# Turning down-projection groups and up-projection tiles of an MLP into one mixed order, with 4 of 8 pairs by seven products

## The chip, the cores and the metric

One core of a Trainium2 chip runs the whole kernel in one launch. The metric is the device time of one execution in microseconds, the median of three runs. Its five engines have queues of their own and meet at semaphores: TensorE (PE; its weight loads are a row of their own, PEld), VectorE (DVE), ScalarE (ACT), GpSimd (POOL) and SyncE (SP, which issues the loads of weights).

## The reference

Two layers over 256 tokens and 2048 features in float32. Each layer is an attention block and then an MLP with a residual:

```python
def rms_norm(x, g):
    xf = x.astype(jnp.float32)
    y = xf * lax.rsqrt(jnp.mean(xf * xf, axis=-1, keepdims=True) + EPS)
    return (y * g.astype(jnp.float32)).astype(x.dtype)

def sq_relu_mlp(h, g, w_in, w_out):
    return jnp.square(jax.nn.relu(rms_norm(h, g) @ w_in)) @ w_out

# in each layer, after attention and its output projection:
#   h = h + sq_relu_mlp(h, norm_mlp[layer], w_mlp_in[layer], w_mlp_out[layer])
# w_mlp_in: 2048 x 8192, w_mlp_out: 8192 x 2048
```

The change is in the MLP alone. The attention, the key and value projections and the output projections stay as they are.

## The kernel before

**Products.** Every matrix product is made from float32 operands split in two parts of a shorter format: `hi` is a cast (ACT), `lo` is the rest (DVE, `lo = raw - hi`). Of the four partial products three are taken, hi·hi, hi·lo and lo·hi. TensorE holds a 128x128 block still and moves up to 512 columns past it. Weights come as units of 128x1024 (512 KB): SP loads `raw`, ACT makes `hi`, DVE makes `lo`. Six `raw`, four `hi` and five `lo` buffers exist. `stream` lists all units in order, `weights()` hands out the next and keeps three more prepared.

**Up.** The MLP goes through four chunks `c` of 2048 hidden features. A chunk has 16 up tiles `f` of 128 features. An up tile takes two weight units and the normed input `xg_` (tile `mlpx`): 16 wide matmuls (`hi` weights still, 512 columns: hi and lo of the 256 tokens) and 16 narrow ones (`lo` weights, 256 columns). `two_tiles` makes two tiles together: the wide ones of both, then the narrow ones of both, or in the opposite order (`width["last"]` keeps the kind that came last, so that kinds change as seldom as possible). `features_major` makes one tile in that way. After the last matmul `low_part` copies the bank's right half (ACT, `low`, L451), `up` adds the left half (DVE, L1132) and squares the relu (DVE, L1138); `finish` multiplies by `r2`, the inverse mean square of the token (DVE, L1093), casts `hid` hi (ACT, L1094) and subtracts for `hid` lo (POOL, L1095). `r2` comes from `inverse_square`: a matmul with minus ones, a scaling and a reciprocal on DVE (L552, L553).

**Down.** When all 16 tiles of a chunk are done, `pair_group(c, n)` multiplies the chunk with the down weights, for `n` = 0 and 1, each 1024 of the 2048 outputs in two columns of 512. Here tokens stand still and weights move, 512 wide. The chunk's 16 tiles make eight pairs `j`. For each pair the block product has two token halves, two feature tiles and two columns. Directly that is 8 products (two weight units, one for each column, 12 matmuls each). By a Strassen-Winograd scheme it is 7 products in four weight steps (21 matmuls): the sums and differences of weights are made in place by DVE (`prepare_seven`, four operations on 512 columns, L222 to L226), those of the hidden values by DVE in `finish` (L1111), and both are split again. The table `SEVEN` says which pairs go by seven: 0, 2, 4 (THREE) or 0, 2, 4, 6 (FOUR), for each layer, chunk and group; `group_order` puts two or three direct units between the steps of a seven-product pair. A group's sums lie in eight PSUM banks: 11, 21, 12 and 22 in the pool `ps_mm` (which has four, shared with all up tiles and other projections), p1 and p5 in `ps_s` (two), p6 in `ps_t` and p7 in `ps_y` (one each). When a sum is complete it is copied (first chunk, mostly by ACT) or added by DVE (L1057) to `d` and `e` tiles in SBUF; in some groups ACT copies it first and DVE adds later (`staged`). `merged` combines the seven sums at the end and `turned` transposes the result on TensorE and adds it to `h` (L998).

In the last chunk only group 0 goes that way; the other two quarters of the outputs are made by `tokens_major`, and in layer 1 the last one by `features_major`.

**Order.** TensorE's instructions stay in program order (`InOrder`). On DVE, ACT and POOL the compiler's scheduler orders the instructions, by readiness and program order, once and for all; each engine then works its queue in that order and waits at the head. Side work (`later`, `start_side`) is placed by `slot()`, which is called once or twice per tile. A tile of a pool takes any free buffer of its tag, and waits if there is none.

Of the kernel before, what the change touches and what calls it, by code (L numbers as in the profile page):

```python
# [16 lines left out]
P = 128  # L17
D = 2048
T = 256
# [33 lines left out]
def group_order(sevens):  # L53


    others = [(j, col) for col in "12" for j in range(KT // 2) if j not in sevens]
    behind = (1, 2, 3) if len(sevens) == 3 else (1, 2)
    steps = []
    for j in sevens:
        for i in range(4):  # L60
            steps.append((j, i))
            if i in behind:
                steps.append(others.pop(0))
    return steps + others
# [41 lines left out]
def trunk(  # L106
# [440 lines left out]
    def inverse_square(acc, name):  # L547

        ps = ps_y.tile([P, 512], F32, name="inv", tag="y")
        mm(ps[:, :T], neg_ones[:], acc[:], True, True)  # L550
        r2 = const.tile([P, T], F32, name=f"r2_{name}", tag="r2")
        nc.vector.tensor_scalar(r2[:], ps[:, :T], -1.0 / D, EPS, op0=ALU.mult, op1=ALU.add)  # L552
        nc.vector.reciprocal(r2[:], r2[:])  # L553
        return r2
# [248 lines left out]
    def mlp_stream(l):  # L803
        for c in range(NCH):
            n = FIRST_UP if c == 0 else 0
            for h in range(2):
                for f in range(n):
                    stream.append(w_up[l, c * KT + f, h])
            for f in range(n, KT):
                for h in range(2):  # L810
                    stream.append(w_up[l, c * KT + f, h])
            def unit(g, j):
                ap = w_down[l, 4 * g : 4 * g + 4, 2 * c + j // 4]
                ap = ap[:, :, 256 * (j % 4) : 256 * (j % 4) + 256]
                return ap.rearrange("o p x -> p o x")

            for n, sevens in enumerate(SEVEN[l][c]):
                for j, step in group_order(sevens):
                    sides = [unit(2 * n + i, j) for i in range(2)]
                    if step == 0:  # L820
                        seven = Sevenfold(*sides)
                    stream.append(Gathered(sides["12".index(step)]) if step in ("1", "2") else seven)
            for g in range(2, 4) if c == NCH - 1 else ():
                if by_features(l, c, g):
                    for o in range(4 * g, 4 * g + 4):
                        for h in range(2):
                            stream.append(w_down[l, o, 2 * c + h])
                    continue
                stream.extend(Gathered(unit(g, j)) for j in range(KT // 2))
# [141 lines left out]
    def mlp(l, xg_, sq, h, done):  # L971
        inv = {}
        later(lambda: inv.update(r2=inverse_square(sq, f"mlp{l}")), 4)
# [50 lines left out]
        def pair_group(c, n, hid, factors, staged=None):  # L1024

            banks = {q: ps_mm.tile([P, 512], F32, name="acc", tag="acc") for q in ("11", "21", "12", "22")}
            banks.update((q, ps_s.tile([P, 512], F32, name="acc", tag="s")) for q in ("p1", "p5"))
            banks["p6"] = ps_t.tile([P, 512], F32, name="acc", tag="t")
            banks["p7"] = ps_y.tile([P, 512], F32, name="acc", tag="y")
            sevens = len(SEVEN[l][c][n])  # L1030
            counts = {q: [0, 3 * sevens] for q in banks}
            for q in ("11", "21", "12", "22"):
                counts[q][1] = 6 * (KT // 2 - sevens) + (3 * sevens if q != "22" else 0)

            sums_of = {
                "11": [summed(0, 2 * n)], "21": [summed(1, 2 * n)],
                "12": [summed(0, 2 * n + 1)], "22": [summed(1, 2 * n + 1)],
                "p1": [product_sum(0, n), summed(0, 2 * n)], "p6": [product_sum(0, n)],
                "p5": [product_sum(1, n)], "p7": [product_sum(2, n)],
            }  # L1040

            def add(q, a, w):
                product(banks[q], a, w, counts[q])
                if counts[q][0] < counts[q][1]:
                    return
                src = banks[q][:]
                if staged is not None and q in ("12", "22", "p1", "p5", "p6", "p7"):
# [3 lines left out]
                    staged.extend((dst, copy[:]) for dst in sums_of[q])  # L1051
                    return
                for dst in sums_of[q]:
                    if c == 0 and q not in ("11", "p6"):
# [4 lines left out]
            def tokens(kt, m):  # L1059
                return [hid[:, kt, i * T + m * P : i * T + (m + 1) * P] for i in range(2)]  # L1060

            def part(unit, k2):
                return [x[:, k2 * 512 : (k2 + 1) * 512] for x in unit]

            for j, step in group_order(SEVEN[l][c][n]):
                w = weights()
                if step in ("1", "2"):
                    for m in range(2):
                        for k2 in range(2):
                            add(f"{m + 1}{step}", tokens(2 * j + k2, m), part(w, k2))  # L1070
                    slot()
                    continue
                s = factors[j]
                pairs = [
                    (("p1", tokens(2 * j, 0)), ("11", tokens(2 * j + 1, 0))),
                    (("12", s[3]),),
                    (("p5", s[0]), ("p7", s[2])),
                    (("p6", s[1]), ("21", tokens(2 * j + 1, 1))),
                ][step]
                for k2, (q, a) in enumerate(pairs):  # L1080
                    add(q, a, part(w, k2))
                if step in (1, 3):
                    slot()

        began = clock["slot"]
        for c in range(NCH):
            hid = new_act(f"hid{l}_{c}")
            squares = {}
            factors = {}

            def finish(f, hid=hid, squares=squares, factors=factors, c=c):
                a = squares[f]
                nc.vector.tensor_tensor(a[:], a[:], inv["r2"][:], op=ALU.mult)  # L1093
                nc.scalar.copy(hid[:, f, :T], a[:])  # L1094
                nc.gpsimd.tensor_tensor(  # L1095
                    hid[:, f, T:], a[:], hid[:, f, :T].bitcast(F32), op=ALU.subtract
                )
                if f % 2 == 0 or f // 2 not in SEVEN[l][c][-1]:
                    return

                s12 = nar.tile([P, T], F32, name="s12", tag="bias", bufs=6)
                s34 = nar.tile([P, T], F32, name="s34", tag="bias", bufs=6)
                a11, a21 = squares[f - 1][:, :P], squares[f - 1][:, P:]
                a12, a22 = a[:, :P], a[:, P:]
                for out_, x0, x1, op in (
                    (s12[:, :P], a21, a22, ALU.add),
                    (s12[:, P:], s12[:, :P], a11, ALU.subtract),
                    (s34[:, :P], a11, a21, ALU.subtract),
                    (s34[:, P:], a12, s12[:, P:], ALU.subtract),
                ):  # L1110
                    nc.vector.tensor_tensor(out_, x0, x1, op=op)  # L1111
                factors[f // 2] = []
                if f // 2 < 6:
                    s_hi = wide.tile([P, 512], F32R, name="s_hi", tag="wide")
                    s_lo = wide.tile([P, 512], F32R, name="s_lo", tag="wide")
                for i, s in enumerate((s12, s34)):
                    if f // 2 < 6:
                        hi, lo = (x[:, i * T : (i + 1) * T] for x in (s_hi, s_lo))
                    else:
                        hi, lo = (  # L1120
                            nar.tile([P, T], F32R, name=name, tag="bias", bufs=6)[:]
                            for name in ("s_hi", "s_lo")
                        )
# [24 lines left out]
            for f in range(n, KT, 2):  # L1148
                two_tiles(xg_, [lambda b, i=i: up(i, b) for i in (f, f + 1)])
# [248 lines left out]
```

## Time and profile before

| | |
|---|---|
| median of 3 runs | 2166.73 us (2166.26 to 2167.32) |
| profiled execution, first to last instruction | 2165.4 us |
| TensorE busy | 2158.2 us, 11083 matmuls |
| VectorE busy | 1690.1 us |
| ScalarE busy | 1191.3 us |
| GpSimd busy | 326.7 us |
| first MLP | from 435.7 to 1126.9 us |
| second MLP | from 1470.6 us to the end |
| TensorE clock granted | 1.000 |

For the profiled execution the span from its first to its last instruction is what was kept of its own time; the timed median is 1.3 us longer. A row of the page's groups, or of the view by line, reads: line, engine, operation, output<-inputs, shapes, count | busy us, mean ns of one | idle us of the engine just before them, and what ended most of it. A row in order of time reads: start us, duration us, engine, line, operation, in brackets the idle time before it and what ended it. A row of waits reads: who <- for whom: us in total, times, longest. TensorE's matmuls are pipelined, so one takes longer than the step from start to start.

### The profile page before, as it was taken

How to read it: one execution, taken by the hardware profiler on the slowest of the kernel's cores; microseconds unless marked ns; L12 is line 12 of the kernel's file. 1: busy time of each engine (PE TensorE's matmuls, PEld its weight loads, DVE VectorE, ACT ScalarE, POOL GpSimd, SP SyncE). 2: the span in 40 equal slices, each digit the busy share in tenths (PEclk: the TensorE clock that was granted, in tenths of full speed). 3: DMA queues.
4: the chain of work that ended last, by engine and by line, in shares of the span. 5: the costliest groups of instructions: out<-in, count | busy, mean ns of one | idle time of the engine just before them, and what ended most of it. 6: DMA issues, size and time to landing. Idle time of an engine off the chain costs nothing.

```text
span 2165.4 us, 30280 instructions
## 1 busy us (share of the span) xinstructions
PE 2158.2 (100%) x11083; PEld 1852.1 (86%) x11083; DVE 1690.1 (78%) x2431; ACT 1191.3 (55%) x1668; POOL 326.7 (15%) x349
## 2 busy tenths in 40 slices
PE   9999999999999999999999999999999999999999
PEld 8888888888888888888888889888888888988887
DVE  7778885678977987997886556567797798799796
ACT  7744545555655555555555447655565556555553
POOL 0010112621001001001050112352100100100100
PEclk9999999999999999999999999999999999999999
DMA  9655556655765765666666654455676577667665
GB/s 325 197 165 185 168 179 195 198 192 166 212 205 178 208 213 178 194 219 189 202 180 191 185 190 136 131 188 183 182 201 224 164 203 223 188 180 219 190 180 156
DMA packets 213317, 414.66 MB, mean 191 GB/s; under 512 B 13232, under 2 KB 144304, under 8 KB 213168
## 3 DMA queue, kind: packets, MB, share of 16 engines
q1 hardware_dynamic: 212592, 410.63, 62.0%
q8 instruction: 87, 1.43, 0.3%
q10 hardware_dynamic: 576, 2.10, 0.3%
q14 instruction: 62, 0.51, 0.1%
HBM read 410.58 MB, written 2.10 MB: 191 GB/s over the span
## 4 chain that ended last, share of the span: by engine, by line
PE 98%; DVE 1%; DMA 0%; issue 0%; ACT 0%; SPq 0%
PE acc L77 94%; PE yp L77 1%; PE accs L77 1%; PE tp L77 1%; PE s L77 1%; PE z L77 1%; DMA raw<-in_w_mem 0%; DVE lo L176 0%; DVE pt L640 0%; DVE lo L250 0%; DVE h L998 0%; ACT hi L173 0%; DVE kvx L465 0%; ACT hi L249 0%; PE stat L77 0%
## 5 line engine op out<-in xcount | busy, mean ns | idle before, releaser
L176 DVE TENSOR_TENSOR lo<-raw,hi 128x1024 fp32r<-128x1024 f32 (+1 forms) x524 | 642.6, 1237 | 308.4 <-ACT hi L173 183.3
L173 ACT CAST hi<-raw 128x1024 fp32r<-128x1024 f32 (+1 forms) x524 | 546.4, 1045 | 375.8 <-PE acc L77 316.7
L77 PE MATMUL acc<-hi,hid 128*128 128x512 f32 x1474 | 481.4, 389 | 0.0
L77 PE MATMUL acc<-mlpx,hi 128*128 128x512 f32 x2048 | 472.6, 390 | 0.0
L77 PEld LDWEIGHTS acc<-mlpx,hi 128*128 128x128 f32 x2048 | 382.0, 188 | 77.7
L77 PEld LDWEIGHTS acc<-hi,hid 128*128 128x128 f32 x1474 | 276.7, 188 | 57.5
L77 PE MATMUL acc<-lo,hid 128*128 128x512 f32 x737 | 286.7, 389 | 0.0
L1095 POOL TENSOR_TENSOR hid<-upsq,hid 128x256 fp32r<-128x256 f32 x128 | 122.3, 964 | 1086.2 <-ACT hid L1094 1086.2
L227 ACT CAST hi<-raw 128x1024 fp32r<-128x1024 f32 x204 | 192.1, 946 | 132.8 <-PE acc L77 56.0
L77 PEld LDWEIGHTS acc<-mlpx,lo 128*128 128x128 f32 x2048 | 250.6, 192 | 2.8
L77 PE MATMUL acc<-mlpx,lo 128*128 128x256 f32 x2048 | 252.0, 283 | 0.0
L228 DVE TENSOR_TENSOR lo<-raw,hi 128x1024 fp32r<-128x1024 f32 x204 | 222.8, 1108 | 29.6 <-ACT hi L227 28.0
L249 ACT CAST hi<-raw 128x1024 fp32r<-128x1024 f32 x146 | 154.0, 1055 | 126.1 <-PE acc L77 104.5
L77 PE MATMUL acc<-hi,xg 128*128 128x512 f32 x640 | 208.4, 398 | 0.0
L250 DVE TENSOR_TENSOR lo<-raw,hi 128x1024 fp32r<-128x1024 f32 x146 | 179.2, 1228 | 14.4 <-ACT hi L249 13.7
L77 PEld LDWEIGHTS acc<-lo,hid 128*128 128x128 f32 x737 | 138.4, 188 | 28.5
L77 PEld LDWEIGHTS acc<-hi,xg 128*128 128x128 f32 x640 | 120.2, 188 | 24.6
L451 ACT COPY low<-acc 128x256 f32<-128x256 f32 x188 | 69.1, 368 | 112.2 <-PE acc L77 111.9
L77 PE MATMUL acc<-lo,xg 128*128 128x512 f32 x320 | 124.7, 390 | 0.7 <-DVE lo L176 0.7
L77 PE MATMUL acc<-y,hi 128*128 128x512 f32 x512 | 119.9, 391 | 0.0
L77 PEld LDWEIGHTS acc<-y,hi 128*128 128x128 f32 x512 | 95.0, 188 | 19.0
L1094 ACT CAST hid<-upsq 128x256 fp32r<-128x256 f32 x128 | 51.9, 407 | 75.6 <-DVE upsq L1093 75.4
(202 smaller groups left out, 2610.4 us busy)
## 6 DMA issues: line engine op xcount, KB each, us to landing
raw<-in_w_up SPq DMA_DIRECT2D x256, 512.0 KB, 4.4
raw<-in_w_down SPq DMA_DIRECT2D x256, 512.0 KB, 5.6
raw<-in_w_in SPq DMA_DIRECT2D x80, 512.0 KB, 3.7
raw<-in_w_o SPq DMA_DIRECT2D x64, 512.0 KB, 4.0
raw<-in_w_mem SPq DMA_DIRECT2D x28, 512.0 KB, 5.9
raw<-in_w_kv_v SPq DMA_DIRECT2D x24, 512.0 KB, 3.9
raw<-in_w_kv_k SPq DMA_DIRECT2D x24, 512.0 KB, 4.2
raw<-in_w_q SPq DMA_DIRECT2D x24, 512.0 KB, 4.1
```

The lines of the kernel that those rows point to most:

```text
L77: return self._tc.keep_in_program_order(fn(*args, **kwargs))
L173: nc.scalar.copy(hi[:, :n], raw[:, :n])
L176: nc.vector.tensor_tensor(lo, raw, hi.bitcast(F32), op=ALU.subtract)
L227: nc.scalar.copy(hi4, src)
L228: nc.vector.tensor_tensor(lo4, src, hi4.bitcast(F32), op=ALU.subtract)
L249: nc.scalar.copy(hi4, turned)
L250: nc.vector.tensor_tensor(lo4, turned, hi4.bitcast(F32), op=ALU.subtract)
L451: nc.scalar.copy(low[:], bank[:, T:])
L1094: nc.scalar.copy(hid[:, f, :T], a[:])
L1095: nc.gpsimd.tensor_tensor(hid[:, f, T:], a[:], hid[:, f, :T].bitcast(F32), op=ALU.subtract)
```

## The change

The MLP's steps are now written as one list, `mlp_steps`. The first two tiles of chunk 0 (H) and the next six (T, by `two_tiles`) come first. Then for each chunk and group `weave` mixes kinds of steps: `U` f is an up tile (by `features_major`), `S` j a pair by seven products, `A` j and `B` j a direct unit of the first or second column. In group 0 of a chunk (`late`) the up tiles are the chunk's own last eight; in group 1 they are the first eight of the next chunk. In every group pairs 0 to 3 go by seven and 4 to 7 directly. The orders that come out are

```
late:  U8 S0 U9 S1 U10 S2 U11 S3 U12 A4 A5 U13 U14 A6 U15 B4 B5 B6 A7 B7
other: U0 S0 A4 U1 S1 A5 U2 S2 A6 U3 S3 A7 U4 U5 B4 U6 B5 U7 B6 B7
last:  (chunk 3 has group 0 only, in the late order)
```

A bank is taken at a sum's first product, and 22 comes from `ps_s`. `hid` is one tile for all chunks of a layer. The inverse is now a root, `ri`, by a power on POOL over 128x256; relu and `ri` are applied together on DVE and ACT squares. The subtraction for `hid` lo moves from POOL to DVE. The block sums of the hidden values get new homes (some in the even tile's place in `hid`), and the even tile of a seven-product pair is no longer split by itself except in the last chunk. In layer 1, `turned(3)` moves behind the last group.

```diff
-THREE, FOUR = (0, 2, 4), (0, 2, 4, 6)
-SEVEN = [
-    [(FOUR, FOUR), (THREE, FOUR), (THREE, FOUR), (THREE,)],
-    [(FOUR, FOUR), (THREE, FOUR), (THREE, FOUR), (FOUR,)],
-]
+SEVEN = [4, 4]
+BY_TURNS = 8
+
+def weave(sevens, late):
+    first, second = [], []
+    u = BY_TURNS if late else 0
+    for j in range(sevens):
+        first += [("U", u), ("S", j)]
+        u += 1
+    direct = list(range(sevens, KT // 2))
+    last = u + BY_TURNS - sevens
+    if late:
+        a, b = list(direct), list(direct)
+        for i, f in enumerate(range(u, last)):
+            second.append(("U", f))
+            while a and 2 * a[0] + 1 < f:
+                second.append(("A", a.pop(0)))
+        second += [("B", j) for j in b[:-1]] + [("A", j) for j in a] + [("B", b[-1])]
+    else:
+        steps, first = first, []
+        a = list(direct)
+        for step in steps:
+            first.append(step)
+            if step[0] == "S" and a:
+                first.append(("A", a.pop(0)))
+        b = [("A", j) for j in a] + [("B", j) for j in direct]
+        for f in range(u, last):
+            second += [("U", f)] + ([b.pop(0)] if f > u else [])
+        second += b
+    return first + second
...
-    def inverse_square(acc, name):
+    def inverse_root(acc, name):
...
-        nc.vector.reciprocal(r2[:], r2[:])
-        return r2
+        nc.gpsimd.tensor_tensor(
+            ri[:], ri[:], neg_half[:, 0:1].to_broadcast([P, T]), op=ALU.pow
+        )
+        return ri
...
+            def bank(self, q):
+                if q not in self.banks:
+                    pool, tag = {
+                        "p1": (ps_s, "s"), "p5": (ps_s, "s"), "22": (ps_s, "s"),
+                        "p6": (ps_t, "t"), "p7": (ps_y, "y"),
+                    }.get(q, (ps_mm, "acc"))
+                    self.banks[q] = pool.tile([P, 512], F32, name="acc", tag=tag)
+                return self.banks[q]
...
-                nc.vector.tensor_tensor(a[:], a[:], inv["r2"][:], op=ALU.mult)
-                nc.scalar.copy(hid[:, f, :T], a[:])
-                nc.gpsimd.tensor_tensor(
-                    hid[:, f, T:], a[:], hid[:, f, :T].bitcast(F32), op=ALU.subtract
+        def split(hi, lo, src):
+            nc.scalar.copy(hi, src)
+            nc.vector.tensor_tensor(lo, src, hi.bitcast(F32), op=ALU.subtract)
...
+        def finish(c, f):
+            squares, factors = chunks[c]
+            a = squares[f]
+            nc.vector.scalar_tensor_tensor(
+                out=a[:], in0=a[:], scalar=0.0, in1=inv["ri"][:], op0=ALU.max, op1=ALU.mult
+            )
+            nc.scalar.activation(a[:], a[:], AF.Square)
+            if f // 2 >= sevens:
+                split(hid[:, f, :T], hid[:, f, T:], a[:])
+            elif f % 2 == 1:
+                split(hid[:, f, :T], hid[:, f, T:], a[:])
+                factors[f // 2] = block_sums(c, f // 2, squares.pop(f - 1), a)
...
+        for c, n, kind, i in mlp_steps(l):
...
+            if kind == "U":
+                features_major(xg_, lambda b, c=c, i=i: up(c, i, b))
+                continue
...
+            if kind == "S":
+                groups[c, n].seven(i)
+            else:
+                groups[c, n].direct(i, "AB".index(kind) + 1)
```

More of the change, by code (lines that the diff above doesn't have):

```diff
@@ L1022, in product @@
                 count[0] += 1
[L1024 to L1044, printed above, removed]
+        hid = new_act(f"hid{l}")
@@ new lines, in seven @@
+            def seven(self, j):
+                s = self.factors[j]
+                width["last"] = "wide"
+                for step, pairs in enumerate((
+                    (("p1", s[0]), ("11", tokens(2 * j + 1, 0))),
+                    (("12", s[4]),),
+                    (("p5", s[1]), ("p7", s[3])),
+                    (("p6", s[2]), ("21", tokens(2 * j + 1, 1))),
+                )):
+                    w = weights()
+                    for k2, (q, a) in enumerate(pairs):
+                        self.add(q, a, part(w, k2))
+                    if step in (1, 3):
+                        slot()
@@ new lines, in direct, with tokens, part @@
+            def direct(self, j, col):
+                width["last"] = "wide"
+                w = weights()
+                for m in range(2):
+                    for k2 in range(2):
+                        self.add(f"{m + 1}{col}", tokens(2 * j + k2, m), part(w, k2))
+                slot()
+        def tokens(kt, m):
+            return [hid[:, kt, i * T + m * P : i * T + (m + 1) * P] for i in range(2)]
+        def part(unit, k2):
+            return [x[:, k2 * 512 : (k2 + 1) * 512] for x in unit]
@@ new lines, in up @@
+        def up(c, f, bank):
+            early = c == 0 and f < 4
+            low = low_part(bank)
+            if early:
+                t = wide.tile([P, T], F32, name="up", tag="wide")
+            else:
+                t = nar.tile([P, T], F32, name="up", tag="nar")
+            chunks[c][0][f] = t
+            nc.vector.tensor_tensor(t[:], bank[:, :T], low[:], op=ALU.add)
+            if early:
+                later(lambda: finish(c, f), began + 11 + f - clock["slot"])
+            else:
+                finish(c, f)
@@ new lines, in down_last, with group @@
+        def down_last(o, bank):
+            nc.vector.tensor_tensor(h(o), bank[:, T:], h(o), op=ALU.add)
+            done(o)
+        def group(g, banks):
+            for m in range(2):
+                nc.vector.tensor_tensor(
+                    summed(m, g), banks[m][:], summed(m, g), op=ALU.add
+                )
+            start_side(turned(g, done))
+        for g in range(2, 4):
+            if not by_features(l, c, g):
+                tokens_major(hid, lambda b, g=g: group(g, b))
+                continue
+            for o in range(4 * g, 4 * g + 4):
+                if o == KT - 1:
+                    last_tile(
+                        hid, lambda b, o=o: down_early(o, b), lambda b, o=o: down_last(o, b)
+                    )
+                else:
+                    features_major(hid, lambda b, o=o: down(o, b))
```

304 lines of the change are left out of this document (128 added, 176 removed).

## The prediction

> **What bounds the kernel now.** I read the head of the page first, then TensorE's waits, then busy time by stage, then the order of time in two places.
>
> ```profile
> span 2165.4 us, 30280 instructions
> PE 2158.2 (100%) x11083; PEld 1852.1 (86%) x11083; DVE 1690.1 (78%) x2431; ACT 1191.3 (55%) x1668; POOL 326.7 (15%) x349
> PE 98%; DVE 1%; DMA 0%; issue 0%; ACT 0%; SPq 0%
> ...
> PE tp L77 <- DVE h L998: 1.9, 2, 1.1
> PE cold L77 <- DVE zeros L144: 1.1, 1, 1.1
> PE acc L77 <- DVE lo L176: 0.7, 1, 0.7
> PE accs L77 <- ACT hi L173: 0.4, 1, 0.4
> ```
>
> TensorE carries 98% of the chain and waits for other engines 4.1 us in all (last four rows), of which the MLPs hold the two `tp` waits. So there is next to no wait to remove: time falls only with TensorE work, and any new wait of TensorE is paid in full. Next, stages (columns: PE, PEld, DVE, ACT, POOL busy, clock, DMA share, GB/s) and TensorE at the start of the first MLP:
>
> ```profile
> 525.00:606.60 81.60, 81.60 (x361) 67.59 (x360) 76.09 (x86) 53.05 (x64) 2.95 (x2) 1.00 0.73 207
> 777.70:866.50 88.80, 88.80 (x513) 78.76 (x512) 67.75 (x108) 47.19 (x71) 12.28 (x14) 1.00 0.60 191
> 866.50:948.80 82.30, 82.30 (x364) 68.16 (x364) 77.31 (x90) 47.90 (x54) 2.81 (x2) 1.00 0.69 204
> 1037.60:1126.90 89.30, 88.18 (x401) 72.83 (x401) 77.96 (x89) 45.24 (x53) 27.17 (x25) 1.00 0.67 200
> ...
> 451.11 14.70 PE L77 MATMUL acc<-mlpx,hi 128*128 128x512 f32 x64
> 465.64 7.83 PE L77 MATMUL acc<-mlpx,lo 128*128 128x256 f32 x64
> 473.31 2.00 PE L77 MATMUL acc<-mlpx,hi 128*128 128x512 f32 x8
> ```
>
> From start to start, 64 wide products take 465.64 - 451.11 = 14.53 us, 0.227 us each, and 64 narrow ones 473.31 - 465.64 = 7.67 us, 0.120 each; the turns from wide to narrow and back lie inside and cost nothing. An up tile is 16 of each: 5.55 us (a sixteenth of the second stage's 88.80). Down groups (first and third stage) run TensorE full with DVE at 93 to 94%; up tiles (second) leave DVE at 76%.
>
> **The change part by part.**
>
> *Products.* A pair with seven products is 21 wide matmuls in place of 24. Before, 25 pairs have them in layer 0 (4+4, 3+4, 3+4, 3) and 26 in layer 1; after, 28 in each. 5 more pairs x 3 x 0.227 = 15 matmuls = -3.4 us. The clock row is 1.00 and no matmul becomes shorter, so this is all that TensorE can gain, bar the two `tp` waits (1.9 us), which I leave as they are: the transposes stand behind the same DVE adds. The Trainium skill (TensorE: Matmul & The Clock Gate, Back-to-back issue gap) gives about 131 ns per matmul at N=512 in a stream with weight loads; by it the 15 would be worth 2.0 us. This trace has 227, and the trace decides.
>
> *A wait for a PSUM bank, new.* Up tiles and the sums 11, 21 and 12 share the four banks of ps_mm. In the late order (U8 S0 U9 S1 U10 S2 U11 S3 U12 A4 A5 U13 U14 A6 U15 B4 B5 B6 A7 B7) 11 and 21 are open from S0 to A7, 12 from S0 to B7: one bank is left for up tiles. Everywhere an S or an A, 4.76 or 2.72 us of matmuls, stands between two up tiles, except U13 and U14. U14's first matmul waits until ACT has copied U13's `low` and DVE has added `up`; TensorE's order is fixed, so A6, U15 and all behind it wait too. In the other order U4 and U5 are neighbours also, but 11 and 21 closed at A7, one tile earlier. There are 4 late groups in each layer: 8 waits. The trace shows the length of that evacuation, where two free banks hide it:
>
> ```profile
> 466.85 2.36 DVE L176 TENSOR_TENSOR lo<-raw,hi 128x1024 fp32r<-128x1024 f32 x2 [3.55 <-issue]
> 467.75 0.37 ACT L451 COPY low<-acc 128x256 f32<-128x256 f32 x1 [0.82 <-PE acc L77]
> 469.13 0.42 DVE L1132 TENSOR_TENSOR up<-acc,low 128x256 f32<-128x256 f32 x1
> ...
> 455.96 0.36 ACT L451 COPY low<-acc 128x256 f32<-128x256 f32 x1
> 457.23 0.42 DVE L1132 TENSOR_TENSOR up<-acc,low 128x256 f32<-128x256 f32 x1
> ```
>
> The first tile of that narrow run issues its 16 until 465.64 + 16 x 0.120 = 467.56; `low` starts 0.19 later, DVE is held by two `lo`, `up` ends at 469.55: 2.0 us. A tile that ended wide issued until 451.11 + 16 x 0.227 = 454.74 and was out at 457.65: 2.9 us, ACT and DVE both held. With both free it is 0.19 + 0.37 + 0.42 = 1.0. Bounds 1.0 and 2.9; I take 2.0, because U13 ends narrow like the first, and A6's and U15's weights are split at just that time. 8 x 2.0 = +16.0 us (8 to 23). Between U14 and U15 A6's 2.72 us cover the 2.0.
>
> *VectorE in the mixed stretches.* Its instructions overlap a little, so I take start to start:
>
> ```profile
> 525.09 1.22 DVE L250 TENSOR_TENSOR lo<-raw,hi 128x1024 fp32r<-128x1024 f32 x1
> 526.23 0.69 DVE L225 TENSOR_TENSOR raw<-raw,raw 128x512 f32<-128x512 f32 x1
> 526.83 1.22 DVE L228 TENSOR_TENSOR lo<-raw,hi 128x1024 fp32r<-128x1024 f32 x1
> 527.97 0.42 DVE L1132 TENSOR_TENSOR up<-acc,low 128x256 f32<-128x256 f32 x1
> 528.30 0.90 DVE L226 TENSOR_TENSOR raw<-raw 128x512 f32<-128x512 f32 x1
> ...
> L1111 DVE TENSOR_TENSOR s<-upsq 128x128 f32<-128x128 f32 x30 | 20.3, 716 | 0.5
> ```
>
> A full `lo` is 1.14, a 512-wide operation 0.60, a 256-wide one 0.33. A pair of seven is 3 x 1.14 + 5 x 0.60 = 6.4 beside 4.76 of TensorE; a direct unit 1.14 beside 2.72. Before, one S goes with two A/B: 8.7 in 10.2. After, late: one S with one up tile, whose three operations stay three (the multiplication by r2 goes to ACT as a Square, the `hid` subtraction comes from POOL): 6.4 + 2 x 1.14 + 3 x 0.33 = 9.7 in 10.3, 94%, four times in a row; then up tiles with A and B at 60%. In the other order U, S and A take 6.4 + 3.4 + 0.7 = 10.5 for an even tile; an odd one has eight operations of 256 elements or fewer besides (a split, four block sums, three splits), two of them perhaps as long as the 0.72 that they took beside POOL: 2 x 0.72 + 6 x 0.33 = 3.4 more, so at most 12.2 in 13.0 on average, 94%. The first quoted stage ran at 93% with no wait, so I put it at nothing; its price without that cover is a rival. The accumulations (9 x 0.60 a group on DVE; in the first chunk ACT copies most) fall into the second halves with room.
>
> *ScalarE, POOL, DMA.* 128 Squares at 0.41 us (row L1094 below) are 52 us of ACT; it stood at 51 to 65% in the stages, so hidden, though Square now stands between two DVE operations of the same tile: the chain to `hid` is longer by about 0.8 us, and A6 first reads U13 5.5 us later. POOL loses 128 `hid` subtractions (row L1095); none of its successors waited, so no gain. Pairs read the same two raw units as their A and B: as many DMAs and bytes; SP issues them in another order, four units in 10.3 us, 203 GB/s, as in the stages above: nothing. `hid` is now one tile for all chunks; U1 writes features 0 and 1 only after S0, and each later writer follows its reader in the same way: nothing.
>
> *The inverse root.* A DVE reciprocal is replaced by a POOL power over 128x256, twice:
>
> ```profile
> 449.86 1.75 DVE L553 RECIPROCAL r_mlp<-r_mlp 128x256 f32<-128x256 f32 x1
> 451.65 0.76 DVE L1093 TENSOR_TENSOR upsq<-upsq,r_mlp 128x256 f32<-128x256 f32 x2
> 453.19 1.05 ACT L173 CAST hi<-raw 128x1024 fp32r<-128x1024 f32 x1 [0.34 <-PE acc L77]
> ...
> L571 POOL TENSOR_TENSOR sroot<-msq,neg_half x20: 1007/1012/1983, 59.5 to 1221.1; 128x4 f32<-128x4 f32 x20
> L483 POOL TENSOR_TENSOR sq<-h 128x256 f32<-128x256 f32 x45 | 48.3, 1078 | 36.0 <-DVE h L964 23.8 <-DVE h L998 12.0
> L1095 POOL TENSOR_TENSOR hid<-upsq,hid 128x256 fp32r<-128x256 f32 x64 | 61.0, 962 | 542.7 <-ACT hid L1094 542.7
> L1094 ACT CAST hid<-upsq 128x256 fp32r<-128x256 f32 x64 | 25.9, 406 | 37.3 <-DVE upsq L1093 37.2
> ```
>
> No row has this power. If its 1.0 us on 4 elements is a start-up, it costs that plus an ordinary 256-wide operation, 2 us; if it goes by element, 1.007 / 4 x 256 = 64 us. Until then DVE, and behind it ACT with its Square, stand still in their queues. TensorE has 64 wide products from 451.1; the second 32, from 458.4, need casts that began at 453.2 and took 1.05: ACT may be 4 us late. The old inverse was ready at 451.6, so a power of up to 5.8 us costs nothing, each us above it about one. I take the low end, since the row of equal shape (1.08) is the near one in size, with the other as a rival. The Trainium skill (GPSIMD Engine Reference, Performance pitfalls for Q7 kernels) says that a chain of dependent fp32 steps costs 4 cycles for each step and element unless unrolled; that speaks for the high end, and no run here shows it.
>
> **Sum.** -3.4 + 16.0 = +12.6 us on the profiled 2165.4: 2178.0. The timed median, 2166.7, lies 1.3 above the span: 2179.3.
>
> **The rivals.**
> (a) Not slower: U13's evacuation comes at once because little else is queued. At 1.0 us a wait the sum is +4.6, 2171.3; if U14 does not wait at all, 2163.3. It decides below 0.96 us a wait, where the total stays within 4.3 us (0.2%, about what a measurement of this kernel can tell from no change). For it: the second half of a late group loads DVE at 60%. Against: splits of coming weights fill any free slot, as in the quoted rows.
> (b) DVE doesn't hold 94% with up tiles between the pairs. If it gets 88% done, a late U and S take 9.7 / 0.88 = 11.0, 0.7 more, 4 x 8 times: +22, 2202. For it: subtraction, cast and `lo` of one pair alternate between DVE and ACT. Against: no wait at 93% before; three units are prepared ahead.
> (c) The power is long: at 64 us (64 - 6) x 2 = +116, 2295; at 15 us +18, 2197. For it the four-element row, against it only the shape.
>
> **How the numbers follow.** Forecast 0.45 (0.04 of it within 4.3 us), (a) 0.17, (b) 0.17, (c) 0.21, half of it above 2220. The forecast's own range is 2171 to 2187; the whole reaches from (a) to past (b) and the short powers of (c): 2163 to 2215. A gain of over 4.3 us needs more than the 3.4 of matmuls, the `tp` waits too: 0.04, out of (a). Within: the other 0.13 of (a) and 0.04 of the forecast, 0.17. Slower: 0.79.
>
> **What would show it.** 15 fewer matmuls (11068). In TensorE's waits eight of 1 to 3 us at `acc`, released by `up`, about 10 us before a late group's end. DVE 90 to 95% busy in late first halves, with no TensorE wait for `lo`. One POOL power a layer; its duration, and whether ACT or DVE stand behind it, settles (c). I am wrong if those eight waits are missing, or if waits for `lo` or `hi` exceed them.

## The result, and the profile after

The changed kernel takes 2220.18 us (2219.22 to 2223.03), the kernel before 2166.7: a ratio of 1.0249, 95% interval 1.0235 to 1.0264. That is 53.4 us slower, against 12.6 forecast, and above the range. The profiled execution spans 2221.3 us against 2165.4, 55.9 more. Lines of the changed kernel named below: `low` L475 and `up` L1186 take an up tile out of its bank; L1168 applies relu and root, L1171 squares; L1126 and L1127 are the two halves of `split`; L246 to L250 make the sums of weights and L252 their low parts; L200 is the low part of an ordinary weight unit; L1039 are the additions of `merged`.

The page: its head, its chain of waits by engine, and one of its groups:

```profile
span 2221.3 us, 30125 instructions
PE 2173.0 (98%) x11068; PEld 1854.9 (84%) x11068; DVE 1678.7 (76%) x2465; ACT 1225.1 (55%) x1784; POOL 286.2 (13%) x223
PE 91%; POOL 4%; DVE 4%; ACT 1%; issue 0%; DMA 0%; SPq 0%; ACTq 0%
...
L577 POOL TENSOR_TENSOR ri_mlp<-ri_mlp,neg_half 128x256 f32<-128x256 f32 x2 | 82.3, 41138 | 14.3 <-DVE ri_mlp L576 14.3
```

TensorE's waits:

```profile
PE acc L101 <- ACT hid L1126: 20.1, 2, 10.1
PE acc L101 <- DVE up L1186: 14.8, 10, 3.8
PE acc L101 <- DVE lo L252: 5.1, 6, 1.5
PE tp L101 <- DVE h L1023: 2.2, 2, 1.1
```

The 15 matmuls are gone. TensorE's share of the chain fell from 98 to 91%; POOL, 0% before, holds 4% by one instruction that ran twice, the power. The first three rows of waits, 40 us, are all new. The place of the largest, in order of time (selected rows):

```profile
450.28 41.14 POOL L577 TENSOR_TENSOR ri_mlp<-ri_mlp,neg_half 128x256 f32<-128x256 f32 x1 [7.14 <-DVE ri_mlp L576]
485.79 0.88 PE L101 MATMUL acc<-mlpx,lo 128*128 128x256 f32 x6
491.45 2.10 DVE L1168 SCALAR_TENSOR_TENSOR up<-up,ri_mlp 128x256 f32<-128x256 f32 x6 [3.57 <-POOL ri_mlp L577]
491.91 1.09 ACT L1171 ACTIVATE up<-up 128x256 f32<-128x256 f32 x3 [5.29 <-DVE up L1168]
496.74 0.79 PE L101 MATMUL acc<-hi,hid 128*128 128x512 f32 x1 [10.07 <-ACT hid L1126]
497.33 0.63 PE L101 MATMUL acc<-lo,hid 128*128 128x512 f32 x1
497.75 1.05 PE L101 MATMUL acc<-hi,hid 128*128 128x512 f32 x2
```

The same place by stretches (selected; columns as in the prediction):

```profile
435.70:486.60 50.90, 50.90 (x295) 45.00 (x293) 29.48 (x34) 21.49 (x27) 41.57 (x7) 1.00 0.60 176
490.00:497.00 7.00, 0.26 (x1) 0.27 (x2) 5.52 (x20) 4.13 (x13) 1.42 (x1) 0.51 0.19 71
497.00:507.00 10.00, 6.49 (x21) 4.78 (x21) 9.93 (x27) 7.82 (x18) 0.00 (x0) 0.83 0.29 70
520.00:545.00 25.00, 24.59 (x127) 20.78 (x127) 23.28 (x31) 16.93 (x25) 0.00 (x0) 1.00 0.72 202
```

Read it from the power down. It runs from 450.3 to 491.4. TensorE works on without a gap until 486.6 (first stretch: 50.90 of 50.90), through all eight first up tiles and U8; then it needs the first pair's hidden values. From the end of the power six relu-and-root operations on DVE, squares, and splits lead to `hid` at 496.74: 5.3 us. So TensorE stands still for 10.1 us. The clock follows: 0.51 in the stretch of the wait, and the next matmul is 0.42 us behind the one before it (497.33 to 497.75), where 0.227 is the full step. Then U9 waits again (3.8 us), since U8's bank is not out yet. VectorE has a backlog there: in the 40 us from 451 to 491 it was busy for 29.4 us in the kernel before and is for 20.5 now, and from 497 to 507 for 9.93 of 10.

To account for the whole I took, for every two neighbouring matmuls of the MLPs, the time from start to start less the full-clock step (0.227 wide, unrounded 0.2267, and 0.120 narrow). This excess is 2.2 us in the kernel before and 60.9 after: 58.7 more, less 3.4 for the products, is 55.3 of the 55.9. A wait counted in this way is a little longer than the idle time in the rows. Of the 60.9, 46.0 are waits, 8.5 steps at half clock and 6.4 small delays. By place: the two powers with the waits and the slow clock behind them 18.1 and 18.5; the eight waits U13 to U14 8.6; the start of chunk 3's group 3.1 of waits in the first layer, 3.5 in the second, with 2.3 of half clock there.

### The profile page after: what moved, and what is told of

Read it like the earlier page. It is cut to its first block, busy times and chain, and to the rows that moved or that the text cites. A ratio compares the mean times of both kernels' runs of the same rounds, so it can differ in the third digit from the quotient of the medians.

```text
span 2221.3 us, 30125 instructions
## 1 busy us (share of the span) xinstructions
PE 2173.0 (98%) x11068; PEld 1854.9 (84%) x11068; DVE 1678.7 (76%) x2465; ACT 1225.1 (55%) x1784; POOL 286.2 (13%) x223
## 4 chain that ended last, share of the span: by engine, by line
PE 91%; POOL 4%; DVE 4%; ACT 1%; issue 0%; DMA 0%; SPq 0%; ACTq 0%
PE acc L101 87%; POOL ri_mlp L577 4%; PE yp L101 1%; PE accs L101 1%; PE tp L101 1%; PE s L101 1%; PE z L101 1%; DVE lo L200 1%; ACT hi L197 1%; DVE lo L252 1%; DMA raw<-in_w_mem 0%; DVE up L1168 0%; ACT hi L251 0%; DVE up L1186 0%; DVE d L1039 0%
## 5 line engine op out<-in xcount | busy, mean ns | idle before, releaser
L200 DVE TENSOR_TENSOR lo<-raw,hi 128x1024 fp32r<-128x1024 f32 (+1 forms) x524 | 641.4, 1236 | 293.8 <-ACT hi L197 261.9
L101 PE MATMUL acc<-hi,hid 128*128 128x512 f32 x1520 | 506.8, 392 | 20.1 <-ACT hid L1126 20.1
L101 PE MATMUL acc<-mlpx,hi 128*128 128x512 f32 x2048 | 489.0, 392 | 7.4 <-DVE up L1186 7.4
L101 PEld LDWEIGHTS acc<-hi,hid 128*128 128x128 f32 x1520 | 287.2, 189 | 78.7 <-ACT hid L1126 20.5
L251 ACT CAST hi<-raw 128x1024 fp32r<-128x1024 f32 x224 | 211.4, 945 | 198.0 <-DVE raw L247 132.6
L101 PE MATMUL acc<-lo,hid 128*128 128x512 f32 x760 | 298.0, 392 | 0.0
L101 PEld LDWEIGHTS acc<-mlpx,lo 128*128 128x128 f32 x2048 | 260.2, 191 | 17.2 <-DVE up L1186 9.0
L101 PE MATMUL acc<-mlpx,lo 128*128 128x256 f32 x2048 | 264.9, 283 | 7.4 <-DVE up L1186 7.4
L252 DVE TENSOR_TENSOR lo<-raw,hi 128x1024 fp32r<-128x1024 f32 x224 | 241.9, 1087 | 36.4 <-ACT hi L251 30.9
L274 DVE TENSOR_TENSOR lo<-raw,hi 128x1024 fp32r<-128x1024 f32 x136 | 167.2, 1231 | 65.8 <-ACT hi L273 65.1
L273 ACT CAST hi<-raw 128x1024 fp32r<-128x1024 f32 x136 | 143.3, 1055 | 93.5 <-PE acc L101 85.8
L101 PEld LDWEIGHTS acc<-lo,hid 128*128 128x128 f32 x760 | 143.9, 189 | 26.6
L475 ACT COPY low<-acc 128x256 f32<-128x256 f32 x188 | 69.4, 369 | 119.4 <-PE acc L101 117.3
L577 POOL TENSOR_TENSOR ri_mlp<-ri_mlp,neg_half 128x256 f32<-128x256 f32 x2 | 82.3, 41138 | 14.3 <-DVE ri_mlp L576 14.3
```

Of the source, the lines that this page charges most:

```text
L101: return self._tc.keep_in_program_order(fn(*args, **kwargs))
L200: nc.vector.tensor_tensor(lo, raw, hi.bitcast(F32), op=ALU.subtract)
L251: nc.scalar.copy(hi4, src)
L252: nc.vector.tensor_tensor(lo4, src, hi4.bitcast(F32), op=ALU.subtract)
L273: nc.scalar.copy(hi4, turned)
L274: nc.vector.tensor_tensor(lo4, turned, hi4.bitcast(F32), op=ALU.subtract)
```

## Experiments

Times are medians, and each ratio is to the kernel before, 2166.6 to 2166.7 in all batches.

**The power away.** Nothing else is changed: ScalarE makes the root in two activations.

```diff
-        nc.gpsimd.tensor_tensor(
-            ri[:], ri[:], neg_half[:, 0:1].to_broadcast([P, T]), op=ALU.pow
-        )
+        nc.scalar.activation(ri[:], ri[:], AF.Ln)
+        nc.scalar.activation(ri[:], ri[:], AF.Exp, scale=-0.5)
```

> The changed kernel, with the inverse root made by two ScalarE activations (logarithm, then exponential of minus one half of it) instead of the power on POOL; all else the same. Theory P (the power holds back the first seven-product pair of each layer): TensorE's steps above their floor between 486 and 546 us and between 1546 and 1600 us in the changed kernel were 18.3 and 18.8 us; they go, and the time falls by 36 to 38 us, to 2182 to 2185. Rival M (the mixed stretches overload DVE anyway and the power only stands where that shows first): under 15 us of gain, above 2205, with waits for DVE's lo in the first mixed stretch instead.

2195.4 us, ratio 1.0134 [1.0118, 1.0149]: 24.8 less, between what the theory and its rival said. The waits for `hid`, 20.1 us, are gone; but at the same place TensorE waits again, in order of time (selected):

```profile
490.94 0.50 PE L101 MATMUL acc<-lo,s_w 128*128 128x512 f32 x1 [0.76 <-DVE lo L252]
494.31 5.49 PE L101 MATMUL acc<-mlpx,hi 128*128 128x512 f32 x16 [1.94 <-DVE up L1185]
```

From start to start, the first pair waits 0.96 us for a low part of its weight sums and U9 2.11 for U8's bank, and a stretch of 3.4 us at half clock follows, in each layer. The power hid a second lateness, which the last experiments take up.

**No neighbouring late up tiles.** One A step behind each of U12, U13 and U14.

```diff
-            while a and 2 * a[0] + 1 < f:
+            if a and 2 * a[0] + 1 < f:
```

> The changed kernel with one direct unit of the first column behind each of U12, U13 and U14 (U12 A4 U13 A5 U14 A6 U15), so that no two up tiles are neighbours while three banks are held; the power stays. Theory B (U14 waits for U13's bank): eight waits of 1.08 us go, 2211 to 2212. Rival: those waits only take up time that DVE and ACT need to catch up, so that it comes back as waits for lo or hi: 2217 to 2221.

2212.0 us, ratio 1.0210 [1.0194, 1.0225]: 8.2 less, as the theory said. Of the ten waits for `up` the two of U9 are left:

```profile
PE acc L101 <- DVE up L1186: 6.4, 2, 3.6
```

The length of the eight is read in the changed kernel, in order of time (selected):

```profile
555.14 2.07 PE L101 MATMUL acc<-mlpx,lo 128*128 128x256 f32 x16
557.25 0.37 ACT L475 COPY low<-acc 128x256 f32<-128x256 f32 x1 [0.86 <-PE acc L101]
557.65 0.42 DVE L1186 TENSOR_TENSOR up<-acc,low 128x256 f32<-128x256 f32 x1
558.13 2.18 PE L101 MATMUL acc<-mlpx,lo 128*128 128x256 f32 x16 [0.92 <-DVE up L1186]
```

U13 issues until 555.14 + 16 x 0.120 = 557.06. ScalarE had been idle for 0.86 us when the tile ended, VectorE follows as soon as the copy is done, and U14 starts at 558.13: 1.07 us.

**Additions of the second sums later.** At the start of chunk 3's group six additions (L1039) run on VectorE between the operations on weight sums.

```diff
-                    start_side(add_second(c))
+                    start_side(delayed(add_second(c), 14))
```

> The changed kernel with the six DVE additions that merge group 1 (add_second) begun 14 slots later, behind S3 of the last group instead of beside S0; the power stays. Theory D (these additions, six of 0.6 us, in front of the weights of S0 cause TensorE's waits for lo in chunk 3, 3.5 us in layer 0 and 6.1 in layer 1, of which about 2.6 are the half clock that follows): 2210 to 2213. Rival (the last chunk's own block sums, split whole, overload DVE there): under 3 us of gain.

2219.7 us, ratio 1.0249 [1.0232, 1.0266]: no gain. The additions were written 14 slots later and came out where they had been. VectorE of this kernel, in order of time (selected):

```profile
1015.63 0.68 DVE L1039 TENSOR_TENSOR d<-d,e 128x512 f32<-128x512 f32 x1
1018.04 0.68 DVE L246 TENSOR_TENSOR raw<-raw 128x512 f32<-128x512 f32 x1
1018.64 0.68 DVE L1039 TENSOR_TENSOR d<-d,e 128x512 f32<-128x512 f32 x1
1019.24 0.68 DVE L247 TENSOR_TENSOR raw<-raw,raw 128x512 f32<-128x512 f32 x1
```

Only TensorE's queue is kept in program order; the compiler moved them ahead again. So whether they cause chunk 3's waits was not tested by this run.

**All three.** 

> All three edits together. If the three losses are separate they add up: 2220.2 - 37.1 - 8.7 - 9.6 = 2164.8, which is 15 matmuls of 0.227 us less than the kernel before, within 2163 to 2167. Rival (one bottleneck moves from wait to wait): above 2172.

2185.5 us, ratio 1.0089 [1.0074, 1.0104]: the rival's side, since the losses do not add up to 2164.8. The excess falls to 22.8 us, 14.2 of it waits. They stand at two seams only: at the first S0 to U9 of each MLP (3.7 us with the 0.58 at a later low part), and at S0 and S1 of chunk 3 (1.70 + 0.42 + 1.03). The late groups of chunks 1 and 2 have none.

**The price of the power.** Six probes on POOL in the kernel with all three edits, whose result nobody reads.

```diff
+            for n in (1, 4, 16, 64, 256):
+                nc.gpsimd.tensor_tensor(
+                    dst[:, :n], inv["ri"][:, :n], neg_half[:, 0:1].to_broadcast([P, n]), op=ALU.pow
+                )
+            nc.gpsimd.tensor_tensor(
+                dst[:, T:], inv["ri"][:], neg_half[:, 0:1].to_broadcast([P, T]), op=ALU.mult
+            )
```

> The kernel of e4 with six operations on idle POOL in layer 0 whose results nobody reads: powers over 128x1, 128x4, 128x16, 128x64 and 128x256, and a multiplication over 128x256. It gives the price by itself. If the power goes by element (41.1 us on 256 less a start of about 0.4): 0.16 us an element, 0.6, 1.0, 3.0, 10.6 and 41 us. If it is a fixed start with some size at which it jumps, the middle two will not lie on that line. The time stays that of e4, 2184 to 2187, since nothing waits for them.

POOL's groups of instructions; L1001 is the power, L1004 the multiplication of the same shape:

```profile
L1001 POOL TENSOR_TENSOR probe<-ri_mlp,neg_half 128x256 f32<-128x256 f32 x1 | 41.1, 41132 | 0.1
L1001 POOL TENSOR_TENSOR probe<-ri_mlp,neg_half 128x64 f32<-128x64 f32 x1 | 10.5, 10538 | 0.1
L1001 POOL TENSOR_TENSOR probe<-ri_mlp,neg_half 128x16 f32<-128x16 f32 x1 | 3.0, 2950 | 0.1
L1004 POOL TENSOR_TENSOR probe<-ri_mlp,neg_half 128x256 f32<-128x256 f32 x1 | 2.4, 2365 | 0.0
L1001 POOL TENSOR_TENSOR probe<-ri_mlp,neg_half 128x4 f32<-128x4 f32 x1 | 2.0, 1990 | 0.0
L1001 POOL TENSOR_TENSOR probe<-ri_mlp,neg_half 128x1 f32<-128x1 f32 x1 | 1.4, 1409 | 40.4 <-DVE hid L1138 40.4
```

From 64 to 256 elements it grows by (41132 - 10538) / 192 = 159 ns for each element of a partition. Drawn back, this line leaves 0.36 us for no element, and it gives 2.9 at 16, as measured. At 4 and 1 it gives 1.0 and 0.5, where the probes took 2.0 and 1.4; this excess of 0.9 to 1.0 us is not explained. So the power goes by element, as expected. The shape alone says nothing: the multiplication takes 2.4 us. The Trainium skill (GPSIMD Engine Reference, Performance pitfalls for Q7 kernels) gives a cost per element for dependent fp32 steps. A cost per element is what these rows show; whether the power is such a chain they do not show. The kernel ran at 2187.2 us in one execution, within the 2184.1 to 2188.8 without probes: a POOL that is busy for 41 us costs little when nobody waits for it.

**TensorE kept busy through the power.** In the changed kernel 44 wide matmuls without use stand ahead of the first S0.

```diff
+                if (c, n, i) == (0, 0, 0):
+                    idle = ps_y.tile([P, 512], F32, name="idle", tag="y")
+                    for _ in range(44):
+                        mm(idle[:], xg_[:, 0, :P], xg_[:, 0, :], True, True)
```

> The changed kernel with 44 wide matmuls more in each layer, into a bank that nobody reads, between U8 and S0 of the first chunk, where TensorE waits 10.1 us for the power; 44 x 0.227 = 10.0 us, so they only fill the wait. If the half clock that the trace shows from 490.1 to 500.4 us comes from the idle time, the clock stays at 1.00 there and about 1.8 us come back in each layer: 2215 to 2218. If the half clock has another cause, or the fill delays S0: 2219 to 2223.

2223.2 us, ratio 1.0264 [1.0248, 1.0280]: no gain in time. Its TensorE in order of time (selected; S0 is from 496.23 to 501.14):

```profile
485.98 10.16 PE L101 MATMUL idle<-mlpx 128*128 128x512 f32 x44
496.23 0.50 PE L101 MATMUL acc<-hi,hid 128*128 128x512 f32 x1
501.14 0.39 PE L101 MATMUL acc<-hi,hid 128*128 128x512 f32 x1
506.52 0.99 PE L101 MATMUL acc<-mlpx,hi 128*128 128x512 f32 x2 [4.99 <-DVE up L1186]
```

Busy time of the stretch behind the power:

```profile
496.00:506.50 10.50, 5.44 (x22) 3.71 (x21) 10.43 (x30) 8.00 (x19) 0.00 (x0) 1.00 0.26 70
```

The clock stays at 1.00 and S0 runs in 5.1 us, so the half clock did come from the idle time. But U9 starts at 506.5, where it had started at 507.1, and by 0.5 of these 0.6 us this run was ahead from the start of the MLP. Half-clock steps fell from 8.5 to 3.1 us, U9's waits grew from 3.8 and 4.0 to 5.2 and 5.8: of 5.4 us 3.2 came back as waits. The two profiled executions differ by 2.7 us in favour of this kernel, the medians by 3.1 the other way, so the rest is not shown as a gain. VectorE is busy for 10.43 of 10.50 us: in this stretch behind the power its backlog sets the time, and a faster S0 mostly waits longer.

**Additions on POOL.** The first two edits, and the six additions of chunk 3 on POOL instead of later.

```diff
-                nc.vector.tensor_tensor(dst, dst, src, op=ALU.add)
+                engine.tensor_tensor(dst, dst, src, op=ALU.add)
...
-            yield from merged(1)
+            yield from merged(1, nc.gpsimd)
```

> As e4, but with the six merging additions of group 1 on POOL instead of begun later on DVE. (Begun later, they were still run beside S0 of the last chunk: the scheduler had moved them up.) If they are what makes S0's lo late in chunk 3, the waits there (1.7, 0.4 and 1.0 us in each layer) go and the time is 2178 to 2180. If the whole block sums are the cause, it stays at 2184 to 2187.

2191.1 us, ratio 1.0114 [1.0101, 1.0128], 5.6 more than all three edits: a miss. VectorE and POOL there, and TensorE's longest wait, in order of time (selected):

```profile
1001.00 1.67 DVE L246 TENSOR_TENSOR raw<-raw 128x512 f32<-128x512 f32 x1
1002.19 1.62 POOL L1038 TENSOR_TENSOR d<-d,e 128x512 f32<-128x512 f32 x1
1002.70 1.66 DVE L247 TENSOR_TENSOR raw<-raw,raw 128x512 f32<-128x512 f32 x1
1003.89 1.61 POOL L1038 TENSOR_TENSOR e<-e,e 128x512 f32<-128x512 f32 x1
1004.40 1.66 DVE L249 TENSOR_TENSOR raw<-raw,raw 128x512 f32<-128x512 f32 x1
1008.91 0.79 PE L101 MATMUL acc<-lo,s_x 128*128 128x512 f32 x1 [2.87 <-DVE lo L252]
```

Beside POOL's additions VectorE's operations on weight sums take 1.66 us, where 0.68 is usual (the rows of the third experiment): the work left VectorE, and the time did not. The Trainium skill (SBUF — State Buffer, Who interferes with whom) says that a VectorE instruction with two SBUF inputs contends with a GpSimd instruction that reads SBUF. The rows agree, and look like taking turns: VectorE's operations end 0.55 us behind POOL's (1004.36 behind 1003.81, 1006.06 behind 1005.50). TensorE's waits there grow from 3.2 to 4.0 us in each layer, and 2.6 and 2.9 us at half clock follow them, which the kernel with all three edits did not have there. So this run does not settle either whether the additions or the block sums make VectorE late in chunk 3.

**The kernel before with seven products in four pairs everywhere.** Its order and all else are as before.

```diff
-    [(FOUR, FOUR), (THREE, FOUR), (THREE, FOUR), (THREE,)],
-    [(FOUR, FOUR), (THREE, FOUR), (THREE, FOUR), (FOUR,)],
+    [(FOUR, FOUR), (FOUR, FOUR), (FOUR, FOUR), (FOUR,)],
+    [(FOUR, FOUR), (FOUR, FOUR), (FOUR, FOUR), (FOUR,)],
```

> The kernel before with one part of the change alone: four pairs by seven products in every group (FOUR instead of THREE at five places), in the old order. The products alone are 15 matmuls: 2163.3, 3.4 us faster. If DVE does not keep up with four pairs in the chunks where it adds from the banks (the old second stage of that kind stood at 94% busy with three and four), waits for lo eat it: 2166 to 2172.

2173.2 us, ratio 1.0031 [1.0019, 1.0042]: 6.6 more, not 3.4 less. TensorE's waits in it, three rows that the kernel before hasn't:

```profile
PE acc L77 <- DVE lo L228: 3.7, 4, 0.9
PE acc L77 <- ACT hi L227: 1.2, 4, 0.3
PE acc L77 <- DVE lo L250: 1.0, 4, 0.2
```

TensorE waits for the parts of weights where the second group of chunks 1 and 2 begins, in both layers. Ahead of the first of these places VectorE is busy for 40.6 of 41.5 us, against 38.6 in the kernel before. In the old order the 15 products saved cost more in VectorE's time than they give.

**The first late group spaced, then the last too, then all.** On top of all three edits, the late order starts with two up tiles: U8 U9 S0 U10 S1 U11 S2 U12 S3 A4 U13 A5 U14 A6 U15 B4 B5 B6 A7 B7, in chunk 0; in 0 and 3; in all four.

```diff
-            for kind, i in weave(SEVEN[l], n == 0):
+            order = weave(SEVEN[l], n == 0)
+            if c in (0, 3) and n == 0:
+                order = [(x[0], int(x[1:])) for x in (
+                    "U8 U9 S0 U10 S1 U11 S2 U12 S3 A4 U13 A5 U14 A6 U15 B4 B5 B6 A7 B7".split()
+                )]
+            for kind, i in order:
```

> The kernel with all three edits (root on ScalarE, at most one A step behind each up tile, additions of the second sums later; 2185.5), and in addition the late order of chunk 0 alone becomes U8 U9 S0 U10 S1 U11 S2 U12 S3 A4 U13 A5 U14 A6 U15 B4 B5 B6 A7 B7: an up tile of 9.8 us more lies ahead of S0, and U9 no longer stands behind S0. Theory (VectorE's and ScalarE's chain behind the root is late for the first products, and U9 waits for U8's bank because the copy of U8 stands late in ScalarE's queue): the waits at the first S0 and U9, 0.8 + 2.0 us in each layer, go, with the steps at half clock behind them: 5 to 7 us less, 2179 to 2181. Rival (the first products wait only because VectorE's work of the whole stretch is more than TensorE's): the wait moves to U10 or S1, and the time stays at 2184 to 2187.

> As the one before, with the same order in chunk 3 too. There S0 and S1 wait 0.4 to 1.7 us three times in each layer for the low parts of the weight sums, beside the six additions of the second sums. Theory (VectorE is behind at the seam of the chunks, and 9.8 us of tile steps ahead of S0 give it time for them): the 3.15 us a layer go, 6 us less than the run before, 2173 to 2175. Rival (the planner uses the new room for other work of VectorE, and the weight sums come as late as before, as when the additions were only started later): as the run before, within 2 us.

> As the one before, with that order in all four late groups. The waits of chunks 1 and 2 are nearly nothing in the kernel with all three edits, so theory (waits at the seams of chunks 0 and 3 are what is left): within 1 us of the run before. Rival (the small losses of a step, 7 us over the whole multi-layer part against 2 in the kernel before, come from the switch of tile and product steps everywhere, and the order in chunks 1 and 2 has part in them): 2 to 4 us less.

2175.9 us (1.0046 [1.0032, 1.0060]), 2169.1 (1.0011 [1.0002, 1.0019]) and 2169.8 (1.0015 [1.0006, 1.0023]). The first step is worth 9.6 us, more than expected: between the profiled executions 6.2 us of waits and 1.7 of half clock are gone, and 0.9 lies ahead of the first MLP. The second is worth 6.8; the third nothing, so its rival falls. What the first removed, in order of time in the kernel with all three edits (selected):

```profile
483.71 2.08 PE L101 MATMUL acc<-mlpx,lo 128*128 128x256 f32 x16
488.84 1.99 ACT L197 CAST hi<-raw 128x1024 fp32r<-128x1024 f32 x2
491.35 0.36 ACT L475 COPY low<-acc 128x256 f32<-128x256 f32 x1
493.05 0.42 DVE L1185 TENSOR_TENSOR up<-acc,low 128x256 f32<-128x256 f32 x1
493.61 3.89 PE L101 MATMUL acc<-mlpx,hi 128*128 128x512 f32 x16 [1.96 <-DVE up L1185]
```

U8 has issued its last matmul at 485.6 and is copied only at 491.35, behind weight casts in ScalarE's queue; VectorE, busy with `lo` parts, adds it at 493.05. With U9 ahead of S0 another bank is free, and S0 comes 5.55 us later, one up tile (not 9.8, as the expectation has it). Which of the two matters more was not tested. What is left with chunks 0 and 3 spaced:

```profile
span 2167.2 us, 30130 instructions
PE tp L106 <- DVE h L1027: 2.2, 2, 1.1
PE acc L106 <- DVE lo L257: 0.8, 2, 0.4
```

Its excess is 7.8 us, 5.6 above the kernel before; less the 3.4 of products that is +2.2, and the spans differ by 1.8. The 5.6 are 1.4 of waits, most of it twice 0.58 at a low part of chunk 0's weight sums, and 4.1 of small delays. No version tried beats the kernel before.

## Why the prediction was wrong, point by point

The sign was right; the size failed in one step, and a second term that was put at nothing added to it. The terms that the sum did have, bank waits less products, make only some 5 of the 53.4 us. Neither of the signs that it named for being wrong came: the eight waits are there (8.6 us), and TensorE's waits for `lo` and `hi` of the pairs' weights (5.6 us by the rows) are below them. The power, which it would look at for rival (c), was the place.

**Products: right.** 11068 matmuls, 0.227 us a step; the excess closes the account with 3.4.

**The inverse root: the step that failed.** It said "I take the low end, since the row of equal shape (1.08) is the near one in size". The shape was no guide to this operation: 41.1 us. The same step also said that ScalarE and VectorE "stand still in their queues" and that 5.8 us are free. That was wrong in the other direction. The compiler had placed the operations that need the root behind the weight work of the time, VectorE waited only 3.57 us for the power, and TensorE had matmuls until 486.6. By these rows a power that ended 5.3 us ahead of that, at 481.3, could have lasted 31 us without a wait for `hid` (an estimate; no run has such a power). So of 41.1 us ten were paid, not (41.1 - 5.8) = 35. Rival (c) had the mechanism and too high a price for each us; even so the two places cost 36.6 us, for U9, the clock and the lateness at the seam come with the ten. Without the power 24.8 us came back.

**The bank wait: right mechanism, mis-sized.** Eight waits, between U13 and U14 and released by `up`, as predicted (though U14 starts 27.6 us before the late group's end, not 10). They last 1.08 us, not 2.0: 8.6 instead of 16.0. The lower bound, "both free", was the case. ScalarE was idle when U13 ended, and VectorE had done its last `lo` when the copy was out, so the row that was taken, where two `lo` held VectorE, was the wrong neighbour; rival (a) had the time of this term and not of the whole.

**VectorE in the mixed stretches: put at nothing, wrong at the seams.** In the middle of a first half the cover held: VectorE is busy for 23.28 of 25 us (93%) after 520, with one wait of 0.58 us, and in the first halves of chunks 1 and 2 (from 672 and from 844) for 39.3 and 39.8 of 41 us, 96 and 97%, with none. At S0 of the first group and at S0 and S1 of chunk 3 it did not. With the power and the bank wait gone 18.9 us remain (22.3 with the products' 3.4); spacing removes 16.4 of them. Rival (b) had nearly the size (22 us) and the wrong place: it spread the loss over 32 pairs, and it sits in four starts, so that the sizes agree by chance. The prediction compared means over a stretch; what failed is the first pair, whose weight sums come late, and in chunk 0 its predecessor's bank too: VectorE and ScalarE enter the stretch behind, and one up tile more ahead of it is enough. What puts VectorE behind at chunk 3 stays open.

**The clock: not in the sum.** It was taken as 1.00. Waits brought 8.5 us at half clock; of the 5.4 us that the idle matmuls took away, 3.2 came back as waits.

Sum of edits on the changed kernel: power -24.8, neighbours -8.2; both with the delayed additions -34.7, which is 1.7 more than the two alone; spacing -9.6 and -6.8: 2169.1. Open: the 4.1 us of small delays in the best version; nothing was tried on them. The moves of work between engines (the square to ScalarE, the subtraction to VectorE) were not taken back one by one either.

## What to carry to other kernels

Price an operation by the row of the same operation at another size before the row of the same shape; where the two differ thirtyfold, as here 2 and 64 us, the choice between them is the forecast, and the measured price can lie between (41.1). Count how long the consumer has other work, from the end of that work back through the chain to the operation, rather than how soon the old result was ready. In an interleaved order look at the seams: here VectorE at 96 and 97% cost no wait in the first halves of chunks 1 and 2, and at 97% (40.7 of 42 us from 1018) chunk 3 began with three, and one more tile ahead of the first step was worth 16.4 us, where all the products saved are worth 3.4.

## What the runs showed of the hardware

A power on POOL costs 159 ns for each element of a partition beside 0.36 us, from 16 elements on. Of the twenty powers on four elements known before the change ten took 1.0 us, which is on this line, and ten 1.5 to 2.0; start-up and elements could not be told apart there. While the long power ran, VectorE was not slowed. Its ordinary `lo` operations from 451 to 491 us, with two inputs in SBUF each, by line (min, median and max in ns, first and last start):

```profile
L200 DVE TENSOR_TENSOR lo<-raw,hi x10: 1216/1224/1226, 454.6 to 478.6; 128x1024 fp32r<-128x1024 f32 x10
```

Their mean over the whole run is 1236. POOL's additions, in the run that had them in chunk 3, slowed VectorE 2.4 times: how long a POOL instruction is does not tell whether it holds VectorE up.

TensorE's clock fell to half 3.5 us into the first layer's 10 us wait, but also behind waits of 0.96 and 2.11 us, 3.4 us apart, in the run without the power. With all three edits the same two waits brought it in the second layer and not in the first. It stayed there for 3.4, 6.8, 10.2 or 13.7 us. The Trainium skill (TensorE: Matmul & The Clock Gate, Part 1: The HAM clock gate) names an idle window of about 3.4 us: the lengths agree, the need for a whole idle one does not.
